# Hyena filters' butterflies in blocks of 64 channels instead of 16, two filter steps per inner tile, and twelve modulation columns beside the output projection

## The chip, the core and the metric

The kernel runs on one core of a Trainium2 chip. The metric is device microseconds from start to end of one execution, the median of several runs. The engines of the core are TensorE (PE, with its weight loads PEld), VectorE (DVE), ScalarE (ACT), GpSimd (POOL) and SyncE (SP). In this kernel SP issues every DMA, in one queue and in its program order (line 50).

## What is computed

One layer of a hybrid diffusion backbone for 1,024 latent and 256 context tokens, width 1,024. The reference, cut to the parts that matter here:

```python
h = x + 1/2 * gate1 * SwiGLU_1(mod1(rms(x)))
h = h + gate2 * W_out[ concat_g norm_g(mixer_g(mod2(rms(h)))) ]   # attention, Hyena, attention, GLA
h = h + 1/2 * gate3 * SwiGLU_2(mod3(rms(h)))
# (shift, scale, gate) x 3 = SiLU(cond) @ W_mod + b_mod : 72 columns of 128 numbers, for latents and for context

def swiglu(x, w_in, w_out):
    a, b = jnp.split(x @ w_in, 2, axis=-1)
    return (jax.nn.silu(a) * b) @ w_out
```

The Hyena mixer is a long convolution by FFT over 256 channels, of order 2. Its filters are implicit: a small MLP of the position gives the taps, and the kernel needs their spectra.

## The kernel before

**Precision and weights.** A product in fp32 is made of three matmuls on operands that are split in a high and a low part (`mm3`, lines 984 to 986: high by high, high by low, low by high). The high part of a weight `wh` is made by ACT (L56), the low part `wl` by POOL or DVE (L62), from a tile `raw` that SP loads. `raw` is a ring of four buffers of 512 KB.

**Stages.** In order of time: `hidden_ctx(0)` and `hidden_lat(0)`, the first half of the first SwiGLU for context and latents; `second(0)`, its second half; projection, Hyena convolution and context attention; linear attention (GLA) and latent attention; the output projection, `w_out(2)` for the context and then `w_out(0)` and `w_out(1)` for the two halves of the latents; then the second SwiGLU with `hidden_ctx(1)`, `hidden_lat(1)` and `second(1)`.

**`hidden_lat`** goes over 22 inner tiles f. Each takes seven products of four chunks by three matmuls of 128x512 (a form of Strassen's: 21 x 4 = 84 matmuls a tile). Between the products DVE adds banks: `u` at L1070, `up1` at L1074 and L1077, `g1` at L1085, and so on. A product that follows in a bank waits for the addition that read it.

**The filters** are a side job of `hidden_lat(0)`: a generator `filters()` from which the loop takes three steps in each inner tile, with high priority. For the latents, after the MLP and the taps, `hyena_spectra` makes four rounds (order `o` by half `g` of 128 channels). A round first makes 8 sub-transforms by matmuls with a DFT matrix (L288, L289), copies and combines them into `sa` and `sd` (ACT L292, DVE L293 and L294), and then runs the butterflies over the 8 sub-transforms, `fft`, in blocks of SW channels. A block takes six operations on POOL (L148 to L153) and ten on DVE (L158 to L163 one each, L166 four), all of which read `sa` and `sd`, and write the block's spectrum to the tile `ks`. That tile has one buffer. It is then stored to `kslat` in DRAM, where each run of SW channels lies by itself. With SW = 16 a round has eight blocks.

**The modulation columns.** `mod_tile(t, sp)` makes column t: it loads 512 KB of `in_wmT`, and DVE multiplies them by SiLU(cond), held in `scb` (1 MB, loaded broadcast and put through a Silu on ACT at L1298), in four accumulating operations (L1311), then adds up (L1313). Columns 16 to 27 are made in `hidden_lat(0)` from f = 10 on, in a pool of one buffer; columns 28 to 71 in `second(0)`. `make_G` and `make_gate` turn columns into the scales and gates that a later stage reads.

**What sets the order.** A scheduler of the framework orders each engine's instructions by priority and dependence. `tc.high_priority(offset=LEAD)` pulls a piece of work ahead of what is written before it; `tc.issue_after(E.last_low)` ties a piece behind the last low split on DVE; `keep_in_program_order` pins an instruction in written order against others of its engine that are pinned. In `w_out` a step loads one weight tile, makes 24 matmuls and evicts the bank with DVE (L1618), which also adds the residual; the result is stored to `hsc2`.

## Time and profile before

| what | value |
|---|---|
| median of 3 runs | 2956.24 us (2952.4 to 2982.59) |
| the profiled execution | 2959.08 us |
| its span in the profile | 2957.3 us |
| mean granted clock of TensorE, share of full speed | 0.961 |
| PE busy | 2749.6 us (93%) |
| PEld busy | 2180.1 us (74%) |
| DVE busy | 1898.0 us (64%) |
| ACT busy | 1133.4 us (38%) |
| POOL busy | 1118.4 us (38%) |
| DMA, mean over the span | 144 GB/s |

Busy shares are means over stages with different limits. PE, busy for 93% of the span, is what the stages mostly wait for, but a stage is only understood from its own rows: how long PE stands still in it, at which granted clock it runs, and which wait ends last. A granted clock of 1.00 is TensorE's level of 2.4 GHz, and a mean below it says that part of the stretch ran at 1.2 GHz.

### The profile page before, as it was taken

The numbers are of one execution on the slowest core, as the hardware profiler recorded it, in microseconds if no ns is written. First come the engines' busy times: TensorE is split into PE (matmuls) and PEld (weight loads), VectorE is DVE, ScalarE is ACT, GpSimd is POOL, SyncE is SP. The second block draws the span as 40 slices with busy tenths as digits, with TensorE's granted clock in tenths as the row PEclk, the third lists the DMA queues.
The fourth block names the chain that finished last, engine by engine and source line by source line (L and its number), as shares of the span: only waits on it lengthen the run. The fifth ranks groups of instructions, "written<-read, shape, count | busy, mean of one in ns | idle before, by whom it ended". The sixth has DMA issues, their size and how long they took to land.

```text
span 2957.3 us, 39868 instructions
## 1 busy us (share of the span) xinstructions
PE 2749.6 (93%) x14088; PEld 2180.1 (74%) x14088; DVE 1898.0 (64%) x3135; ACT 1133.4 (38%) x2051; POOL 1118.4 (38%) x980
## 2 busy tenths in 40 slices
PE   7899988899999888888988989989899999999998
PEld 5886776678788787776754544477898888878888
DVE  4978677754899955767657666662956555533447
ACT  5742222223333642224424434553743333333444
POOL 1334355544000214546415425463435555520002
PEclk9999999999999999899978979999999999999999
DMA  8654755342877563342462110264652222244445
GB/s 296 214 179 139 210 111 125 79 150 93 281 250 263 175 209 113 121 138 84 140 167 50 37 40 12 85 234 157 216 173 97 85 77 84 86 175 149 145 138 202
DMA packets 278460, 427.02 MB, mean 144 GB/s; under 512 B 97417, under 2 KB 163954, under 8 KB 276852
## 3 DMA queue, kind: packets, MB, share of 16 engines
q1 hardware_dynamic: 278260, 424.47, 44.6%
q8 instruction: 111, 1.82, 0.3%
q14 instruction: 89, 0.73, 0.1%
HBM read 345.14 MB, written 79.13 MB: 143 GB/s over the span
## 4 chain that ended last, share of the span: by engine, by line
PE 43%; DVE 5%; DMA 2%; issue 1%; ACT 1%; POOL 1%; SPq 0%; DVEq 0%; POOLq 0%; ACTq 0%
PE ps L986 11%; PE ps L984 10%; PE ps L985 10%; PE ps L740 2%; PE ps L762 1%; PE ps L688 1%; PE ps L763 1%; PE ps L550 1%; PE ps L535 1%; DVE wl L62 1%; DMA gd<-zf 1%; DVE mx L692 1%; PE ps L786 0%; PE ps L546 0%; PE ps L1139 0%
## 5 line engine op out<-in xcount | busy, mean ns | idle before, releaser
L56 ACT ACTIVATE wh<-raw 128x512 fp32r<-128x512 f32 x661 | 408.7, 625 | 513.6 <-PE ps L986 225.0
L62 POOL TENSOR_TENSOR wl<-raw,wh 128x512 fp32r<-128x512 f32 x221 | 328.1, 1489 | 558.1 <-ACT wh L56 342.1
L62 DVE TENSOR_TENSOR wl<-raw,wh 128x512 fp32r<-128x512 f32 x440 | 331.7, 760 | 170.9 <-ACT wh L56 113.2
L985 PE MATMUL ps<-gs,wh 128*128 128x512 f32 (+1 forms) x1056 | 376.5, 357 | 7.0 <-DVE gs L62 7.0
L986 PE MATMUL ps<-gs,wl 128*128 128x512 f32 (+1 forms) x1056 | 373.8, 356 | 2.9 <-DVE wl L62 2.9
L984 PE MATMUL ps<-gs,wh 128*128 128x512 f32 (+1 forms) x1056 | 351.8, 358 | 9.6 <-ACT gs L56 5.0
L984 PE MATMUL ps<-xh,wh 128*128 128x256 f32 (+2 forms) x952 | 320.8, 337 | 12.2 <-ACT zev L1404 5.6
L986 PE MATMUL ps<-xh,wl 128*128 128x256 f32 (+2 forms) x952 | 319.6, 337 | 10.9 <-POOL wl L62 6.4
L985 PE MATMUL ps<-xl,wh 128*128 128x256 f32 (+2 forms) x952 | 323.3, 340 | 0.0
L984 PE MATMUL ps<-t,wh 128*128 128x512 f32 x704 | 281.0, 399 | 11.0 <-DVE up L1077 6.2
L986 PE MATMUL ps<-t,wl 128*128 128x512 f32 x704 | 280.2, 399 | 1.9 <-DVE wl L62 1.9
L985 PE MATMUL ps<-t,wh 128*128 128x512 f32 x704 | 280.5, 398 | 0.0
L984 PE MATMUL ps<-b,wh 128*128 128x512 f32 x528 | 212.6, 403 | 20.6 <-DVE up L1074 19.7
L984 PEld LDWEIGHTS ps<-gs,wh 128*128 128x128 f32 x1056 | 200.3, 190 | 40.7 <-ACT gs L56 5.4
L985 PEld LDWEIGHTS ps<-gs,wh 128*128 128x128 f32 x1056 | 200.9, 190 | 35.9 <-DVE gs L62 7.7
L986 PEld LDWEIGHTS ps<-gs,wl 128*128 128x128 f32 x1056 | 200.5, 190 | 32.4 <-DVE wl L62 3.7
L56 ACT ACTIVATE wh<-s 128x512 fp32r<-128x512 f32 x176 | 110.4, 630 | 295.3 <-PE ps L985 152.1
L985 PE MATMUL ps<-b,wh 128*128 128x512 f32 x528 | 211.5, 401 | 0.0
L986 PE MATMUL ps<-b,wl 128*128 128x512 f32 x528 | 210.9, 399 | 0.2 <-POOL wl L62 0.2
L984 PEld LDWEIGHTS ps<-xh,wh 128*128 128x128 f32 (+1 forms) x952 | 182.3, 192 | 37.5 <-ACT zev L1404 7.2
L986 PEld LDWEIGHTS ps<-xh,wl 128*128 128x128 f32 (+1 forms) x952 | 181.8, 191 | 37.2 <-POOL wl L62 9.1
L919 POOL TENSOR_TENSOR tmp<-tmp 128x512 f32<-128x512 f32 (+1 forms) x18 | 24.7, 1374 | 482.1 <-ACT tmp L917 482.1
(369 smaller groups left out, 5906.5 us busy)
## 6 DMA issues: line engine op xcount, KB each, us to landing
raw<-in_w SPq DMA_DIRECT2D x308, 512.0 KB, 3.5
stg<-in_wmT SPq DMA_DIRECT2D x56, 512.0 KB, 4.1
hid<-g SPq DMA_DIRECT2D x88, 256.0 KB, 2.0
g<-hid SPq DMA_DIRECT2D x88, 256.0 KB, 2.7
m<-in_dft_lat SPq DMA_DIRECT2D x128, 128.0 KB, 2.7
raw<-in_wo SPq DMA_DIRECT2D x24, 512.0 KB, 3.8
x<-in_xT SPq DMA_DIRECT2D x36, 256.0 KB, 4.5
stg<-in_wmp SPq DMA_DIRECT2D x16, 512.0 KB, 10.6
```

The lines of the kernel that those rows point to most:

```text
L56: nc.scalar.activation(out=hi, in_=src, func=ACTF.Copy)
L62: low = eng.tensor_tensor(out=lo, in0=src, in1=hi.bitcast(F32), op=ALU.subtract)
L535: nc.tensor.matmul(ps[:, t], lhsT=kt[32 * h:32 * h + 32, ts], rhs=qt[32 * h:32 * h + 32, ts], start=True, stop=True, tile_position=(32 * h ...
L550: nc.tensor.matmul(ps[:, i0:i0 + 64], lhsT=S[64 * p:64 * p + 64, c], rhs=qt[64 * p:64 * p + 64, 64 * c:64 * c + 64], start=False, stop=c % ...
L688: nc.tensor.matmul(ps, lhsT=qs, rhs=k1[:, lo:hi], start=True, stop=mo is None)
L692: nc.vector.tensor_reduce(out=mx[:, hh * nqt + t, bi:bi + 1], in_=ps, axis=AX.X, op=ALU.max)
L740: mm = nc.tensor.matmul(O[64 * hh:64 * hh + 64, s], lhsT=V[:, kt], rhs=p[hh], start=j == 0, stop=j == last)
L762: nc.tensor.matmul(ps, lhsT=k1[:, ks], rhs=q1[:, hh, a:b], start=True, stop=False)
L763: nc.tensor.matmul(ps, lhsT=k2[:, ks], rhs=q2[:, hh, a:b], start=False, stop=not banded)
L984: nc.tensor.matmul(ps, lhsT=wh(k), rhs=xh(k), start=start and k == 0, stop=False, skip_group_check=loose)
L985: nc.tensor.matmul(ps, lhsT=wh(k), rhs=xl(k), start=False, stop=False, skip_group_check=loose)
L986: nc.tensor.matmul(ps, lhsT=wl(k), rhs=xh(k), start=False, stop=stop and k == nk - 1, skip_group_check=loose)
```

## The change

Blocks of the latents' butterflies have 64 channels, so a round has two blocks instead of eight; an operation is four times as wide, and a store of `ks` has 512 KB in runs of 256 bytes instead of 128 KB in runs of 64. The loop takes two steps of the side job per inner tile instead of three. No modulation columns are made in `hidden_lat(0)`: columns 16 to 59 are made in `second(0)`, 60 to 63 beside `w_out(2)` and 64 to 71 beside `w_out(0)`, from tiles in the ring `raw` that the weights use. For these `scb` is loaded and put through Silu a second time, pinned, ahead of `w_out(2)`. The calls of `make_G` and `make_gate` move accordingly.

```diff
+    def both_conds(p):
+
+        t = p.tile([128, 2, 1024], F32, name="scb")
+        E.load(t, i["cond"].partition_broadcast(128))
+        tc.keep_in_program_order(nc.scalar.activation(out=t, in_=t, func=ACTF.Silu))
+        return t
+
     ms = ExitStack()
     mp = pool(ms, "mp", 1, **R_)
-    scb = mp.tile([128, 2, 1024], F32, name="scb")
-    E.load(scb, i["cond"].partition_broadcast(128))
-    tc.keep_in_program_order(nc.scalar.activation(out=scb, in_=scb, func=ACTF.Silu))
+    scb = both_conds(mp)
...
-    def mod_tile(t, sp):
-
-        w = sp.tile([128, 1024], F32, tag="stg", name="stg")
+    def mod_tile(t, sp, mp=mp, scb=scb, tag="stg"):
+
+        w = sp.tile([128, 1024], F32, tag=tag, name="stg")
...
-    SEQS = (("lat", slice(0, T_LAT), 8, 128, 16), ("ctx", slice(T_LAT, T_ALL), 2, 256, 128))
+    SEQS = (("lat", slice(0, T_LAT), 8, 128, 64), ("ctx", slice(T_LAT, T_ALL), 2, 256, 128))
...
-    sps = ExitStack()
-    sp = pool(sps, "sp", 1, **R_)
     nmod, side_job = 16, filters()
+    nff1 = 60
     for f, _ in enumerate(run):
         with tc.high_priority(offset=LEAD):
-            for _ in range(3):
+            for _ in range(2):
                 next(side_job, None)
-            if f >= 10:
-                mod_tile(nmod, sp)
-                nmod += 1
     for _ in side_job:
         pass
-    sps.close()
...
         for f, _ in enumerate(second(P, 0, c, hid[0], h[c])):
-            if nmod < 72:
+            if nmod < nff1:
                 with tc.issue_after(E.last_low):
                     mod_tile(nmod, sp)
                 nmod += 1
+                if nmod == 24:
+                    make_gate(0)
                 if nmod == 40:
                     make_G(1)
-                    make_gate(0)
-                if nmod == 72:
-                    make_G(2)
-                    make_gate(1)
...
+    mp2 = pool(h2st, "mp2", 1, **R_)
     Y = load_y(2, xp2)
-    for _ in w_out(2, Y, "g", lambda d: h2[:, d]):
+    scb2 = both_conds(mp2)
+
+    def columns(steps, upto):
+
+        nonlocal nmod
+        for t in steps:
+            if nmod < upto:
+                with tc.issue_after(E.last_low):
+                    mod_tile(nmod, P["raw"], mp2, scb2, "raw")
+                nmod += 1
+            yield t
+
+    for _ in columns(w_out(2, Y, "g", lambda d: h2[:, d]), 64):
         pass
+    make_G(2)
...
-            sum_rsq(P, w_out(c, Y[c], "l", lambda d: hq.tile([128, 512], F32, tag="hq", name="hq")), 512, Rl[c],
+            sum_rsq(P, columns(w_out(c, Y[c], "l", lambda d: hq.tile([128, 512], F32, tag="hq", name="hq")), 72), 512, Rl[c],
                     lambda: hq.tile([128, 512], F32, tag="hq", name="rs"))
+    make_gate(1)
```

The following rows show the order of instructions at three places (line of the kernel, operation, out<-in with buffer numbers, shape). A line below the change is a few numbers higher or lower in the new file.

DVE within `hidden_lat(0)`, in the stretch of the butterflies; `u` and `up1` belong to the inner tile, the other names to the filters. Before:

```order
L1074 TENSOR_TENSOR up1_3688<-ps_3647,u_3673 128x512
L163 TENSOR_TENSOR sd_3130<-fP_3593,sd_3130 128x2x16
L166 SCALAR_TENSOR_TENSOR ks_3561<-sd_3130,fA_3570 128x2x16 x2
L166 SCALAR_TENSOR_TENSOR ks_3561<-sd_3130 128x2x16 x2
L158 TENSOR_TENSOR fA_3592<-sd_3130 128x32
L1077 TENSOR_TENSOR up1_3688<-ps_3648,up1_3688 128x512
L159 TENSOR_TENSOR sd_3130<-sd_3130 128x2x16
L162 TENSOR_TENSOR sd_3130<-sd_3130,fP_3593 128x2x16
L160 TENSOR_TENSOR fP_3759<-sd_3130 128x32
L161 TENSOR_TENSOR sd_3130<-sd_3130 128x2x16
L163 TENSOR_TENSOR sd_3130<-fP_3759,sd_3130 128x2x16
L166 SCALAR_TENSOR_TENSOR ks_3583<-sd_3130,fA_3592 128x2x16 x2
```

Now, at the second block of a round:

```order
L159 TENSOR_TENSOR sd_3415<-sd_3415 128x2x64
L163 TENSOR_TENSOR sd_3415<-fP_3834,sd_3415 128x2x64
L162 TENSOR_TENSOR sd_3415<-sd_3415,fP_3834 128x2x64
L62 TENSOR_TENSOR wl_3126<-s4_3123,wh_3125 128x512
L166 SCALAR_TENSOR_TENSOR ks_3824<-sd_3415,fA_3833 128x2x64 x2
L166 SCALAR_TENSOR_TENSOR ks_3824<-sd_3415 128x2x64 x2
L62 TENSOR_TENSOR wl_3130<-raw_3095,wh_3129 128x512
L1070 TENSOR_TENSOR u_3329<-ps_3301,u_3329 128x512
L293 TENSOR_TENSOR sa_3990<-ps_3992,sd_3991 128x2x2x128
L62 TENSOR_TENSOR wl_3270<-s2_3267,wh_3269 128x512
L294 TENSOR_TENSOR sd_3991<-ps_3992,sd_3991 128x2x2x128
L1074 TENSOR_TENSOR up1_3344<-ps_3303,u_3329 128x512
```

The L166 that writes `ks`, which waits for the store of the block before, still stands ahead of the inner tile's L1070 and L1074, but there is one such place in a round and not seven.

PE at the end of the latent attention (L740, L786, and the norm's L801) and the start of `w_out(2)` (L984 to L986, 128x256). Before:

```order
L985 MATMUL ps_17514<-xl_17471,wh_17506 128x256
L986 MATMUL ps_17514<-xh_17470,wl_17507 128x256
L984 MATMUL ps_17514<-xh_17470,wh_17510 128x256
L985 MATMUL ps_17514<-xl_17471,wh_17510 128x256
L786 MATMUL ps_17420<-acc_17249,ones128_87 64x512
L740 MATMUL ps_17251<-p_17405,V_16530 64x512
L740 MATMUL ps_17251<-p_17410,V_16530 64x512
L986 MATMUL ps_17514<-xh_17470,wl_17511 128x256
L984 MATMUL ps_17514<-xh_17470,wh_17510 128x256
L985 MATMUL ps_17514<-xl_17471,wh_17510 128x256
```

And now:

```order
L740 MATMUL ps_16572<-p_16731,V_15851 64x512
L786 MATMUL ps_16741<-acc_16570,ones128_87 64x512
L786 MATMUL ps_16741<-acc_16571,ones128_87 64x512
L801 MATMUL ps_16751<-sq_16752,ones128_87 128x512
L984 MATMUL ps_16841<-xh_16794,wh_16833 128x256
L985 MATMUL ps_16841<-xl_16795,wh_16833 128x256
L801 MATMUL ps_16751<-sq_16755,ones128_87 128x512
L986 MATMUL ps_16841<-xh_16794,wl_16834 128x256
L984 MATMUL ps_16841<-xh_16794,wh_16833 128x256
```

The matmuls of `w_out(2)` stood between those of the attention's last block, and now begin behind all of it. On ACT the cause is seen: the pinned Silu of the second `scb` (L1298), with table loads, stands behind the attention's last work and ahead of the first weight split (L56 of `wh`) of `w_out(2)`:

```order
L789 ACTIVATE r_16744<-ps_16741 128x512
L56 ACTIVATE xh_16794<-yr_16816 128x256
L56 ACTIVATE xh_16794<-yr_16820 128x256
L790 ACTIVATE r_16744<-r_16744 128x512
L56 ACTIVATE xh_16794<-yr_16824 128x256
L800 ACTIVATE sq_16752<-y_16356 128x512
L1298 ACT_TABLE_LOAD
L1298 ACTIVATE scb_16828<-scb_16828 128x2048
L56 ACTIVATE wh_16833<-raw_16831 128x512
```

Before, the splits of those weights stood between the exponentials of the attention's last block, ahead of L789.

SP in `w_out(0)`, the queue of loads and stores. Before:

```order
L50 DMA raw_17971<-in_wo 128x1024
L50 DMA hq_18269<-hsc_83 128x512
L50 DMA hsc2_17465<-h2_17469 128x256 x2
L50 DMA raw_18012<-in_wo 128x1024
L50 DMA hsc2_17465<-h2_17469 128x256
L50 DMA raw_18053<-in_wo 128x1024
```

And now:

```order
L50 DMA raw_17401<-in_wo 128x1024
L50 DMA hsc2_16786<-h2_16790 128x256
L50 DMA stg_17440<-in_wmT 128x1024
L50 DMA hsc2_16786<-h2_16790 128x256
L50 DMA raw_17454<-in_wo 128x1024
L50 DMA stg_17493<-in_wmT 128x1024
```

Between two weight loads there is now a load of a modulation column, into the same ring.

## Rows read from the trace of the kernel before

**Rows 1.** Windows by stage; busy us, clock granted, DMA share, GB/s

```profile
core 0: us, PE busy (x) PEld busy (x) DVE busy (x) ACT busy (x) POOL busy (x), PEclk, DMA share, GB/s
191.00:744.00 553.00, 511.37 (x2188) 401.15 (x2188) 373.97 (x760) 143.56 (x244) 267.70 (x348) 0.97 0.46 131
360.00:580.00 220.00, 189.13 (x842) 152.66 (x840) 159.69 (x408) 50.31 (x88) 121.01 (x238) 0.94 0.47 108
2201.00:2636.00 435.00, 434.90 (x1848) 348.95 (x1848) 229.85 (x247) 136.14 (x228) 231.02 (x152) 1.00 0.25 85
1915.00:1954.00 39.00, 31.02 (x208) 24.66 (x206) 32.74 (x35) 21.57 (x42) 29.36 (x20) 1.00 0.91 324
1954.00:2062.00 108.00, 106.77 (x432) 81.31 (x433) 36.65 (x45) 45.68 (x79) 50.33 (x42) 0.98 0.48 161
```

**Rows 2.** Waits from 191 to 744 us: total us, times, longest us

```profile
POOL ks L150 <- DMA kslat<-ks: 87.7, 23, 8.0
DVE ks L166 <- DMA kslat<-ks: 49.1, 24, 4.7
PE ps L984 <- DVE up L1074: 19.7, 6, 5.0
```

**Rows 3.** Timeline of PE, 394 to 402 us: start, us, line, [idle before <-releaser]

```profile
395.80 0.77 PE L984 MATMUL ps<-b,wh 128*128 128x512 f32 x1 [4.91 <-DVE up L1074]
...
399.56 0.40 PE L984 MATMUL ps<-b,wh 128*128 128x512 f32 x1
```

**Rows 4.** DVE groups by shape, 191 to 744 us: busy, mean ns | idle before

```profile
L1311 DVE SCALAR_TENSOR_TENSOR junk<-stg,scb 128x512 bf16<-128x512 f32 x51 | 40.5, 795 | 17.3 <-DMA stg<-in_wmT 16.6 <-ACT scb L1298 0.4
L166 DVE SCALAR_TENSOR_TENSOR ks<-sd 128x32 f32<-128x32 f32 x64 | 23.8, 409 | 0.0
L166 DVE SCALAR_TENSOR_TENSOR ks<-sd,fA 128x32 f32<-128x32 f32 x64 | 17.6, 315 | 49.1 <-DMA kslat<-ks 49.1
L159 DVE TENSOR_TENSOR sd<-sd 128x32 f32<-128x32 f32 x32 | 16.5, 516 | 0.4
...
L162 DVE TENSOR_TENSOR sd<-sd,fP 128x32 f32<-128x32 f32 x32 | 9.8, 305 | 0.7
...
L1313 DVE SCALAR_TENSOR_TENSOR mod<-part,b_mod 128x2 f32<-128x2 f32 x12 | 4.8, 403 | 0.2
...
L1311 DVE DVE_READ_ACCUMULATOR junk<-stg,scb 128x1 f32 x50 | 3.9, 78 | 0.0
```

**Rows 5.** DVE groups by shape, 1545 to 1915 us

```profile
L557 DVE TENSOR_TENSOR o<-ps,o 128x128 f32<-128x128 f32 x20 | 5.8, 291 | 15.2 <-PE ps L550 15.0
```

**Rows 6.** DMA issues: count, KB each, us to landing

```profile
stg<-in_wmT SPq DMA_DIRECT2D x56, 512.0 KB, 4.1
m<-in_dft_lat SPq DMA_DIRECT2D x128, 128.0 KB, 2.7
raw<-in_wo SPq DMA_DIRECT2D x24, 512.0 KB, 3.8
kslat<-ks SPq DMA_DIRECT2D x32, 128.0 KB, 3.4
scb<-in_cond SPq DMA_DIRECT2D x1, 1024.0 KB, 7.0
```

**Rows 7.** Timeline of ACT at 2019 us, a table load

```profile
2019.14 1.28 ACT L894 ACT_TABLE_LOAD   x1
```

**Rows 8.** ACT groups by shape, 190 to 680 us: the Silu of `scb`

```profile
L1298 ACT ACTIVATE scb<-scb 128x2048 f32<-128x2048 f32 x1 | 1.9, 1922 | 2.2 <-DMA scb<-in_cond 2.2
```

**Rows 9.** Timeline of DVE in `w_out(0)`: two evictions that follow each other

```profile
1994.81 0.75 DVE L1618 SCALAR_TENSOR_TENSOR hq<-ps,mod,hq 128x512 f32<-128x512 f32 x1 [5.72 <-PE ps L986]
2001.28 0.75 DVE L1618 SCALAR_TENSOR_TENSOR hq<-ps,mod,hq 128x512 f32<-128x512 f32 x1 [5.71 <-PE ps L986]
```

**Rows 10.** Timeline of POOL at 1920 us: eight low splits in a row

```profile
1920.32 12.26 POOL L62 TENSOR_TENSOR wl<-raw,wh 128x512 fp32r<-128x512 f32 x8
```

## Prediction, made before the changed kernel had run

> **What bounds the kernel now.** I read the windows view by stage first, because a share of the whole span mixes stages with different limits. The same kind of stage stands there twice [rows 1]: `hidden_lat(0)`, with the filters beside it, from 191 to 744 us (553.0 us), and `hidden_lat(1)`, without them, from 2201 to 2636 us (435.0 us). Both hold the same 1,848 matmuls of the three-product chain; the second has PE busy for 434.90 of its 435.00 us at a granted clock of 1.00. So without a side job the stage is purely PE's. In the first the surplus is 118 us. It splits as follows: PE idle 553.00 − 511.37 = 41.6 us; clock 0.97 instead of 1.00, that is 0.03 × 553 = 16.6 us; the rest, some 60 us, is the filters' own matmuls, which the change leaves as they are. What the change can give back in this stage is therefore at most 41.6 + 16.6 = 58 us.
>
> Where is the idle time? From 360 to 580 us PE is idle for 220.00 − 189.13 = 30.9 us and the clock is 0.94 [rows 1]. This is where the filters' butterflies run. The waits view gives the cause [rows 2]: DVE waits 24 times, 49.1 us in all, for the store `kslat<-ks` to leave the only `ks` tile, and PE waits 19.7 us in 6 long stalls for DVE's `up` (L1074). The timeline shows one link of it [rows 3]: PE stands still for 4.91 us in front of a matmul that needs `up`. DVE itself is busy 159.7 of these 220 us and stands 49.1 us at `ks`: 208.8 of 220. So here DVE sets the pace, a third of it by waiting, and PE pays 30.9/49.1 = 0.63 us for each us of that wait.
>
> **The change, part by part.**
>
> *Wider blocks.* A block of 16 channels costs DVE ten operations, 320 for 32 blocks. The two L166 rows have 23.8 + 17.6 us, the six rows L158 to L163 (16.5 us the dearest, 9.8 the cheapest) 69.8: together 111 us [rows 4]. With 64 channels there are 8 blocks, 80 operations of 128 columns. The trace has a DVE operation of that size at 291 ns [rows 5], no dearer than the narrow ones at 305 to 516: what is paid here is paid per instruction. So 80 × 0.29 = 23 us, and 80 × 0.516 = 41 us if the strided forms stay dear. DVE is relieved of 70 to 88 us; POOL in proportion, but it waits 87.7 us for the same store [rows 2] and nobody waits for it.
>
> *The waits on `ks`.* One of the blocks in each round now shares the tile with the one before it, so the waits fall from 24 to about 4 (the second block of each of 4 rounds; the first has a whole round of matmuls ahead of it). A wait now has a mean of 49.1/24 = 2.05 us, 1.35 less than the landing of 3.4 us [rows 6]. The new store is four times as large, 512 KB in 2,048 runs of 256 bytes, where the old has 128 KB in 2,048 runs of 64. Small runs cost little in these rows: 128 KB in few long runs (`m<-in_dft_lat`) takes 2.7 us, and 512 KB in long runs 3.8 to 4.1. I take 4.1. Four waits of 4.1 − 1.35 = 2.75 us are 11 us of DVE, and by 0.63 that is 7 us of PE. In order, the waiting L166 now stands ahead of L1070 and L1074 in one of the places shown, so what waits behind it is again `u` and `up`, and PE behind them: the wait is rarer, not harmless. PE's other idle time in the stage, 41.6 − 30.9 = 10.7 us, I leave as it is. So 41.6 − 7 − 10.7 = **24 us** gained.
>
> Beside this stands a rule. The Trainium skill ("DMA: Bandwidth & Descriptors", section "Specifications") states a minimum transfer of 512 bytes for line rate, below which the DMA engine reads, modifies and writes; the new 256-byte runs are still below it. The rows speak against a large effect (64-byte runs cost 0.7 us more than long ones at 128 KB), but no transfer of 512 KB in such runs is in the trace; what it would mean is the second rival, and the sum by it 2961 us.
>
> *Clock.* The matmul right behind the stall of [rows 3] takes 0.77 us, one 3.76 us later 0.40 us: PE runs slower for some microseconds after it has stood still. Over the stretch the granted clock is 0.94, against 1.00 in the undisturbed stage [rows 1]. With about a sixth of the waits I expect half of the 16.6 us back, **8 us**; the bounds are 0 and 16.6.
>
> *The twelve columns.* One takes four products of 0.795 us, four accumulator reads of 0.078 and one of 0.403, so 3.9 us of DVE [rows 4], 47 us for twelve. They leave the last 12 of the 22 tiles of `hidden_lat(0)`, where they stand beside and behind the butterflies; that helps DVE there, but what PE can gain by it is already counted in the idle time. They come back at the output projection.
>
> *Side job at two steps a tile.* The filters come to 65 steps before (24 blocks more) and 41 after; at three a tile the first fill 21.7 of the 22 tiles, at two the second 20.5. So the spread over the tiles stays as it was, PE's work too, and I cost it at nothing; without that room, steps left over would run with no matmuls of the tiles beside them, at most the 60 us of the filters' own. `second(0)` makes 44 columns in both kernels, numbered differently: nothing.
>
> *Output projection for the context (`w_out(2)`, 1915 to 1954 us).* The DMA already moves 324 GB/s at a share of 0.91 [rows 1]. Added are the second load of the conditioning, 1 MB, and four columns of 512 KB: 3.1 MB, 9.7 us at that rate. At the same time ACT gets a pinned Silu of 1.92 us [rows 8] and three more table loads of 1.28 us [rows 7], 5.8 us in front of the first weight split, and order shows that matmuls of `w_out(2)` no longer fill the tail of the attention. If both lie side by side the price is the larger; if PE covers all but the table loads it is 3.8, and one after the other it is 15.5. I take **9.7 us**: the row has a DMA that is nearly full.
>
> *Output projection for the latents.* Eight columns are 31 us of DVE in the 54 us of `w_out(0)`, where DVE now has about half of 36.65 us in 108 [rows 1]: 49 of 54, tight but under. An eviction (L1618) comes every 6.47 us, and DVE waits 5.7 us ahead of it [rows 9]; a column of 3.9 us fits in that gap. The DMA goes from 161 GB/s to about 240, under the 324 just seen. I take **3 us** (0 to 8).
>
> *Sum*, against the profiled execution's 2959.08 us: −24 − 8 + 9.7 + 3 = −19.3, so 2939.8. The median of the runs is 2956.24, 2.8 lower; on its scale that is **2937 us**.
>
> **The rivals.**
>
> *The stage gains nearly everything.* If the waits that are left fall where DVE has room, idle time and clock come back but for some 6 us: 58 − 6 = 52 gained, 13 lost, so 2956 − 39 = 2917. For it speaks that DVE's load falls by over 110 us, against it that the waiting L166 stands ahead of L1074.
>
> *The large store is slow.* If the landing grows with the bytes at small runs, it takes 4 × 3.4 = 13.6 us. Four waits of 13.6 − 1.35 = 12.2 us are 49 us again, exactly what DVE waits now; the stage then keeps its idle time and its clock and gains only what DVE's relief gives elsewhere, between 0 and 24 (I take 8, as DVE waits rather than works in those stalls). 2956 + 13 − 8 = 2961. It is the time that the Trainium skill's rule on small transfers, named above, would bring. Against it: 2.7, 3.8 and 4.1 us in [rows 6].
>
> *The other side: the shared ring at the output projection.* The columns are loaded into the same ring of four buffers as the weights of `w_out`, and SP issues in order: a column's buffer that DVE hasn't yet read holds back the next weight load and all behind it. With two buffers for weights a load has two steps, 2 × 6.47 = 12.9 us, less its landing of 4.1 [rows 6]; once DVE is more than 8.8 us late, each of the 8 steps waits for a landing: 8 × 4.1 = 33 us. Loss 9.7 + 3 + 33 = 46 against 32 gained: 2956 + 14 = 2970. For it: DVE is 49 of 54 us full, and POOL needs 1.53 us for each half of a weight [rows 10] before that buffer is free. Against it: the eviction has 5.7 us of room, so lateness doesn't add up.
>
> *Order's remainder.* The scheduler also arranges the latent attention and the linear attention beside it differently; the trace gives that no price, so it only widens the range by some 5 us either way.
>
> **How the numbers follow.** The sum's case 0.50, with its own range of 2923 to 2951 (idle and clock terms 15 to 45 together, the output projection 4 to 20); nearly everything gained 0.22; the slow store 0.14; the ring 0.14. The predicted time is that of the first. The range must leave out no more than 2 in 10: it runs from 2908 (lower third of the second case left out) to 2969 (about half of the ring case and the top of the slow store left out). A measurement of this kernel can tell about 1%, 29.6 us, from no change: faster means under 2926.7, slower over 2985.8. Faster: 0.9 of the 0.22, and a quarter of the 0.50, so 0.32. Slower: 0.4 of the ring case, if more than the 8 steps wait, and 0.2 of the slow store, if waits grow beyond those of now: 0.08. Within: 0.60.
>
> **What would show it.** Right: DVE's waits on `ks` fall from 24 to about 4 and from 49 to near 11 us; `kslat<-ks` lands in about 4 us; the DVE operations of L158 to L166 are near 0.3 us; PE idle in `hidden_lat(0)` is near 18 us at a clock of 0.98 or 0.99; the stretch of `w_out(2)` is some 10 us longer, that of `w_out(0)` some 3. Wrong: a landing above 10 us (slow store); PE waiting on `wh` or `raw<-in_wo` at each step of `w_out(0)` (ring); an idle time in `hidden_lat(0)` under 10 us (all gained); or a difference in stages where order shows none.

## The result and the profile after

The changed kernel takes **2923.41 us** (median of 4 runs, 2915.49 to 2929.44). Against the runs of the kernel before the ratio is 0.988, with a 95% interval of 0.985 to 0.991: some 1.2% faster. I had forecast 2937, with 2908 to 2969. The range held and so did the direction, but 13.6 us too little was forecast, and the stages show that this small miss is the difference of larger ones. By the bound that the prediction set itself (faster means under 2926.7 us) the result is "faster", which had 0.32, and not "within", which had 0.60.

The stages as the timelines give them, from the first or last matmul of one to that of the next (profiled executions, spans 2957.3 and 2922.5 us):

| stage | before | after | difference | forecast |
|---|---|---|---|---|
| `hidden_lat(0)` with the filters | 555.6 | 502.2 | −53.4 | −32 |
| `second(0)` | 326.6 | 331.2 | +4.6 | 0 |
| projection, Hyena, context attention | 404.4 | 398.7 | −5.7 | 0 |
| linear and latent attention, first to last L740 | 442.2 | 419.2 | −23.0 | 0 (±5) |
| last L740 to the first matmul of `hidden_lat(1)` | 281.2 | 321.9 | +40.7 | +12.7 |
| `hidden_lat(1)` and `second(1)` | 742.7 | 742.4 | −0.3 | 0 |

The 4.6 and −5.7 us of the second and third rows nearly cancel; where they come from was not looked into.

The windows of the changed kernel that answer to [rows 1] (columns as there): `hidden_lat(0)`, `hidden_lat(1)`, and the stretch after the attention in two pieces.

```profile
193.00:696.00 503.00, 492.54 (x2189) 392.57 (x2190) 284.82 (x418) 146.17 (x245) 244.55 (x205) 1.00 0.42 130
...
2165.00:2602.00 437.00, 434.63 (x1848) 349.00 (x1848) 231.02 (x251) 137.59 (x229) 231.10 (x152) 1.00 0.25 85
...
1852.00:1900.00 48.00, 28.40 (x146) 24.43 (x147) 41.79 (x69) 28.78 (x44) 22.01 (x15) 0.68 0.94 345
1900.00:1955.00 55.00, 46.14 (x200) 35.94 (x199) 54.30 (x98) 22.86 (x45) 35.81 (x28) 0.90 0.56 184
```

In `hidden_lat(0)` PE is now idle for 10.5 us, not 41.6, and the clock is 1.00. In the stretch of `w_out(2)` it is the other way round: PE is busy for 28.40 of 48 us, at a clock of 0.68, with DVE busy for 41.79.

The waits of the changed kernel in `hidden_lat(0)`, which answer to [rows 2] (us in total, times, longest):

```profile
DVE ks L166 <- DMA kslat<-ks: 6.4, 4, 2.7
```

The 24 waits are 4, as forecast, and take 6.4 us where I had put 11; PE's stalls on `up` (L1074), 6 before and 19.7 us, are one of 2.5 us. The store lands in 5.1 us, where I had taken 4.1 (DMA issues: count, KB each, us to landing, as in [rows 6]):

```profile
stg<-in_wmT SPq DMA_DIRECT2D x56, 512.0 KB, 3.7
raw<-in_wo SPq DMA_DIRECT2D x24, 512.0 KB, 4.8
...
kslat<-ks SPq DMA_DIRECT2D x8, 512.0 KB, 5.1
```

### The profile page after: what moved, and what is told of

Read it like the earlier page. It is cut to its first block, busy times and chain, and to the rows that moved or that the text cites. A ratio compares the mean times of both kernels' runs of the same rounds, so it can differ in the third digit from the quotient of the medians.

```text
span 2922.5 us, 39427 instructions
## 1 busy us (share of the span) xinstructions
PE 2732.5 (93%) x14088; PEld 2176.7 (74%) x14088; DVE 1851.9 (63%) x2895; ACT 1143.4 (39%) x2055; POOL 1087.7 (37%) x836
## 4 chain that ended last, share of the span: by engine, by line
PE 42%; DVE 6%; DMA 2%; ACT 1%; issue 1%; SPq 1%; POOL 0%; DVEq 0%; ACTq 0%; POOLq 0%
PE ps L986 11%; PE ps L984 10%; PE ps L985 10%; PE ps L740 2%; DVE junk L1316 2%; PE ps L688 1%; PE ps L762 1%; PE ps L763 1%; SPq L50 1%; PE ps L550 1%; PE ps L535 1%; DMA stg<-in_wmT 1%; PE ps L546 0%; PE ps L786 0%; DMA q<-ml 0%
## 5 line engine op out<-in xcount | busy, mean ns | idle before, releaser
L56 ACT ACTIVATE wh<-raw 128x512 fp32r<-128x512 f32 x661 | 407.9, 625 | 541.6 <-PE ps L986 242.9
L986 PE MATMUL ps<-gs,wl 128*128 128x512 f32 (+1 forms) x1056 | 376.3, 358 | 2.0 <-DVE wl L62 2.0
L984 PE MATMUL ps<-gs,wh 128*128 128x512 f32 (+1 forms) x1056 | 353.8, 359 | 8.7 <-ACT gs L56 5.0
L984 PE MATMUL ps<-xh,wh 128*128 128x256 f32 (+2 forms) x952 | 325.7, 342 | 18.0 <-DVE mod L1318 8.3
L986 PE MATMUL ps<-xh,wl 128*128 128x256 f32 (+2 forms) x952 | 323.9, 341 | 8.6 <-DVE wl L62 6.8
L984 PE MATMUL ps<-t,wh 128*128 128x512 f32 x704 | 278.4, 395 | 4.5 <-ACT wh L56 4.5
L986 PE MATMUL ps<-t,wl 128*128 128x512 f32 x704 | 277.6, 395 | 0.0
L56 ACT ACTIVATE wh<-s 128x512 fp32r<-128x512 f32 x176 | 110.7, 632 | 309.3 <-PE ps L985 150.5
L984 PEld LDWEIGHTS ps<-gs,wh 128*128 128x128 f32 x1056 | 200.2, 191 | 40.6 <-ACT gs L56 5.2
L62 DVE TENSOR_TENSOR wl<-s,wh 128x512 fp32r<-128x512 f32 x132 | 120.2, 911 | 172.1 <-PE ps L985 95.6
L986 PEld LDWEIGHTS ps<-gs,wl 128*128 128x128 f32 x1056 | 200.8, 191 | 32.1 <-DVE wl L62 2.6
L984 PEld LDWEIGHTS ps<-xh,wh 128*128 128x128 f32 (+1 forms) x952 | 185.8, 195 | 43.4 <-ACT wh L56 12.5
L984 PE MATMUL ps<-b,wh 128*128 128x512 f32 x528 | 208.3, 394 | 2.5 <-DVE up L1074 2.5
L986 PEld LDWEIGHTS ps<-xh,wl 128*128 128x128 f32 (+1 forms) x952 | 184.5, 194 | 33.5 <-DVE wl L62 8.8
L985 PE MATMUL ps<-b,wh 128*128 128x512 f32 x528 | 208.8, 395 | 0.0
L986 PE MATMUL ps<-b,wl 128*128 128x512 f32 x528 | 208.5, 395 | 0.0
```

Source lines behind the costliest of these rows:

```text
L56: nc.scalar.activation(out=hi, in_=src, func=ACTF.Copy)
L62: low = eng.tensor_tensor(out=lo, in0=src, in1=hi.bitcast(F32), op=ALU.subtract)
L984: nc.tensor.matmul(ps, lhsT=wh(k), rhs=xh(k), start=start and k == 0, stop=False, skip_group_check=loose)
L985: nc.tensor.matmul(ps, lhsT=wh(k), rhs=xl(k), start=False, stop=False, skip_group_check=loose)
L986: nc.tensor.matmul(ps, lhsT=wl(k), rhs=xh(k), start=False, stop=stop and k == nk - 1, skip_group_check=loose)
```

## The experiments

They take the three stages that moved apart: which part of the change gave the 53 us, where the 23 come from, and what the 41 at the output projection consist of. Stages of all runs, in us, measured as in the table above:

| run | `hidden_lat(0)` | attention | last L740 to `hidden_lat(1)` | median | ratio to before (95%) |
|---|---|---|---|---|---|
| before | 555.6 | 442.2 | 281.2 | 2959.2 | |
| the change | 502.2 | 419.2 | 321.9 | 2923.4 | 0.988 (0.985 to 0.991) |
| columns moved, 16 channels | 538.8 | 418.5 | 321.1 | 2962.1 | 1.002 (0.999 to 1.005) |
| 32 channels, columns in place | 521.8 | 433.2 | 282.5 | 2923.2 | 0.988 (0.984 to 0.993) |
| 64 channels, columns late | 516.8 | 433.7 | 282.5 | 2911.3 | 0.986 (0.980 to 0.992) |
| the change, 56 columns in `second(0)` | 502.0 | 430.9 | 294.4 | 2921.0 | 0.988 (0.983 to 0.992) |
| the change, loads only | 502.7 | 434.3 | 303.8 | 2920.4 | 0.989 (0.984 to 0.994) |
| the change, products only | 503.1 | 420.9 | 311.2 | 2910.1 | 0.987 (0.982 to 0.993) |
| the change, no second Silu | 505.1 | 417.5 | 318.7 | 2925.1 | 0.990 (0.987 to 0.993) |
| 64 channels, columns split 4 and 8 | 507.0 | 445.2 | 287.9 | 2921.0 | 0.989 (0.987 to 0.990) |
| 64 channels, columns late, behind the low split | 502.7 | 434.0 | 282.1 | 2897.8 | 0.981 (0.977 to 0.985) |
| 64 channels, twelve columns left out | 502.6 | 440.4 | 281.4 | 2897.1 | 0.980 (0.977 to 0.983) |
| the change once more | 503.9 | 420.7 | 324.2 | 2924.7 | 0.990 (0.987 to 0.993) |

Each ratio is against runs of the kernel before on the same chip; the stages are those of one profile each. Wide blocks with the columns where they were is not among the runs. What wide blocks give without columns is the difference of two rows, the columns moved with 16 channels and the change: 538.8 − 502.2 = 36.6 us. They differ in the steps per tile too, which the run without columns shows to make no difference.

**Columns moved, with the second conditioning that they need, and nothing else.**

```diff
-    SEQS = (("lat", slice(0, T_LAT), 8, 128, 64), ...
+    SEQS = (("lat", slice(0, T_LAT), 8, 128, 16), ...
-            for _ in range(2):
+            for _ in range(3):
                 next(side_job, None)
```

(against the changed kernel)

> The kernel before with the twelve columns moved and nothing else: blocks of 16 channels, three steps per tile. Theory (three separate terms: wider blocks -53 us in hidden_lat(0), a different order of the attention -21, the columns +37 at the output projection): the attention stands in the same order as in the changed kernel, so it is some 20 us shorter; the output projection some 37 us longer; hidden_lat(0) at most 10 us shorter, since the 24 waits on ks are all still there; in all 2965 us (2955 to 2975). Rival (what helped hidden_lat(0) is that the columns left it): hidden_lat(0) 25 us shorter or more, in all under 2950.

Measured 2962.1 us, no difference from before that can be told. The attention is 23.7 us shorter and the output projection 39.9 longer, both as the theory had it. `hidden_lat(0)` is 16.8 us shorter, between the two forecasts. The waits on `ks` there stand almost as before, the stalls on `up` are fewer (us in total, times, longest):

```profile
DVE ks L166 <- DMA kslat<-ks: 43.8, 23, 4.3
PE ps L984 <- DVE up L1074: 10.6, 4, 3.5
```

So the columns' leaving has a share of its own in the 53 us: 16.8. Where it comes from is seen in the trace of the kernel before. The program makes these columns from f = 10 on, but with the high priority of the side job they run much earlier (products by tile, 191 to 700 us: ns least, median and most, first and last start):

```profile
L1311 DVE SCALAR_TENSOR_TENSOR junk<-stg,scb x48: 671/684/1776, 200.8 to 319.7; 128x512 bf16<-128x512 f32 x48
```

That is in the first six of the 22 inner tiles, and the first operation of a butterfly starts behind it, at 351 us. The same 70 us of the stage, 29 us after its start, in the kernel before and with the columns moved (columns as in [rows 1]):

```profile
220.00:290.00 70.00, 63.07 (x237) 45.68 (x236) 58.06 (x109) 16.66 (x29) 31.37 (x21) 0.98 0.41 136
```

```profile
223.50:293.50 70.00, 70.00 (x259) 49.12 (x257) 40.23 (x55) 17.88 (x30) 27.76 (x22) 1.00 0.40 128
```

PE is idle for 6.9 us beside the columns and for none without them. Over the whole stage its idle time falls from 44.2 to 32.5 us and its busy time, for the same matmuls, from 511.4 to 506.4. The other 5 us of idle time go later in the stage, where no column ran; why is open. For the whole kernel the moved columns by themselves win nothing.

**Blocks of 32 channels, columns where they were.**

```diff
-    SEQS = (("lat", slice(0, T_LAT), 8, 128, 16), ...
+    SEQS = (("lat", slice(0, T_LAT), 8, 128, 32), ...
```

> The kernel before with blocks of 32 channels; the columns stay where they were, three steps per tile. Theory (the number of waits on ks and of operations sets the loss): 12 waits in place of 24, 160 operations in place of 320; hidden_lat(0) 25 to 40 us shorter, attention and output projection as before, in all 2925 us. Rival (the columns' leaving is what helps): under 15 us shorter, 2945 or more.

Measured 2923.2 us, `hidden_lat(0)` 33.8 us shorter: the theory. DVE's waits on `ks` are 16.4 us in 9 times, where 12 times were expected. One number changed gives as much as the whole change, since nothing is paid at the output projection.

**Blocks of 64, columns late in `hidden_lat(0)`.**

```diff
-    SEQS = (("lat", slice(0, T_LAT), 8, 128, 16), ...
+    SEQS = (("lat", slice(0, T_LAT), 8, 128, 64), ...
...
             for _ in range(3):
-                next(side_job, None)
-            if f >= 10:
-                mod_tile(nmod, sp)
-                nmod += 1
+                done = next(side_job, True)
+            if done and sp is None:
+                sp = pool(sps, "sp", 2, **R_)
+            for _ in range(2 if sp is not None else 0):
+                if nmod < 28:
+                    mod_tile(nmod, sp)
+                    nmod += 1
```

(against the kernel before, in part; in the loop over the inner tiles, with its high priority; the output projection as before)

> Blocks of 64 channels, three steps per tile; the twelve columns stay in hidden_lat(0), but two per tile behind the last step of the filters, in a pool of two buffers that is opened then; nothing is made at the output projection. Theory: hidden_lat(0) about 50 us shorter than before, since DVE has room in tiles without filters (47 us of columns in some 8 tiles of 20 us, of which DVE has 10 free each); the attention stands in the order of before and takes as long as before; the output projection as before; in all 2909 us (2900 to 2915). Rival (columns beside the inner tiles cost PE time wherever they are): hidden_lat(0) at most 30 us shorter, 2930 or more.

Measured 2911.3 us, output projection and attention as in the run with 32 channels. The total is the theory's; `hidden_lat(0)`, at 516.8 us, misses its 505 and is 14.6 longer than in the changed kernel, 1.2 us a column. What they do there is seen in the run with the columns behind the low split.

**All 56 columns in `second(0)`, second conditioning kept.**

```diff
-    nff1 = 60
+    nff1 = 72
```

(against the changed kernel, as are the next three)

> The changed kernel with all 56 columns in second(0), none at the output projection; the second conditioning is still loaded and put through its pinned Silu. Theory: the output projection loses at most 10 us against before (Silu, its table loads, 1 MB) where it lost 37; second(0), where DVE has 285 us of 325 and gets 47 more, is 10 to 30 us longer; in all 2905 to 2925 us. Rival (the Silu and the attention tail that is no longer filled are the loss): the output projection still 25 us or more longer than before, in all over 2930.

Measured 2921.0 us. Without a column beside it, the stretch behind the attention is still 13.2 us longer than before, a little more than the 10 expected, and 27.5 shorter than in the changed kernel. So the second conditioning costs about 13, the columns about 27. What the move into `second(0)` saves there is paid elsewhere: `second(0)` is 8.7 us longer than before, and the stage behind it 7.0. The attention stands in an order of its own here, and 40 us of it ran at a mean clock of 0.62 (1804 to 1844 us).

**Loads only, and products only.** In the first the four products of the twelve columns are left out, in the second their loads:

```diff
+        if tag == "raw":
+            w = sp.tile([128, 1024], F32, tag=tag, name="stg")
+            E.load(w, i["wmT"][t - 16])
+            nc.vector.scalar_tensor_tensor(out=mod[:, t], in0=w[:, 0:2], ...)
+            return
```

```diff
+        if tag == "raw":
+            w = scb.rearrange("p c k -> p (c k)")[:, :1024]
+        else:
...
```

> The changed kernel with the four products of each of the twelve columns at the output projection left out: the 512 KB are loaded into the shared ring as before, and one small operation reads them, so these columns are not the real ones. From the last L740 to the start of hidden_lat(1) the kernel before takes 281 us, the changed one 322, and one with the second conditioning and no columns 294. Theory (DVE: its products, four to a column, stand ahead of the evictions and of the low splits): 295 to 302 us, in all 2900 us. Rival (ring and DMA: a column's load takes a weight's buffer): 312 to 322 us, in all 2918 us.

> The changed kernel with the loads of the twelve columns at the output projection left out: the products are made on data that is already there (the second conditioning), so these columns are not the real ones, and the ring holds weights alone. Theory (DVE): 312 to 322 us from the last L740 to hidden_lat(1), in all 2918 us. Rival (ring and DMA): 294 to 302 us, in all 2900 us. About 305 here and in the run with loads alone would say that it takes both.

Measured 303.8 us with loads alone and 311.2 with products alone, where 294.4 is the stretch with the conditioning only and 321.9 the whole. So the loads cost 9.4, the products 16.8, together 26.2 of 27.5: it takes both, nearly as a sum, the products the larger part. Neither theory holds alone. The medians can't show these parts, as the four runs of each kernel scatter over 31 and 36 us; they rest on one profile each, and the changed kernel's own stretch came out 2.3 us apart in two profiles.

**The Silu left out.**

```diff
-    scb2 = both_conds(mp2)
+    scb2 = both_conds(mp2, False)
```

> The changed kernel with the second Silu left out (the conditioning is loaded and used as it is, so twelve columns are not the real ones). It tells what the pinned Silu with its table loads costs, beside the loads. Theory (the tail of the attention can be filled again and two table loads go): 322 - 8 = 314 us from the last L740 to hidden_lat(1), in all 2915 us. Rival (the columns behind it are the bound, the Silu is hidden in front of them): 320 us or more, in all 2922 us.

Measured 318.7 us for the stretch, 3.2 shorter; the median, 2925.1, can't be told from the changed kernel's. The stretch lies between the theory's 314 and the rival's 320, nearer the rival: the Silu itself is nearly hidden. By difference some 10 of the 13 us are left for the 1 MB load and for the tail of the attention, which `w_out(2)` doesn't fill in this run either; the two were not taken apart.

**Columns split, four late in `hidden_lat(0)`, eight in `hidden_lat(1)`.**

```diff
+    for f, _ in enumerate(hidden_lat(P, 1, XL, hid[1])):
+        if 4 <= f and nmod < 72:
+            with tc.high_priority(offset=LEAD):
+                mod_tile(nmod, sp2, mp2, scb2)
...
```

(the part in `hidden_lat(1)`; four columns late as above)

> A version meant to be faster than both: blocks of 64 channels, three steps per tile; four columns late in hidden_lat(0), 44 in second(0), and the last eight (gate 3, not read until second(1)) in hidden_lat(1), which has DVE busy for 230 us of 435 and a DMA share of 0.25, with a conditioning of its own. Against the run with all twelve late in hidden_lat(0), 2911 us, theory (columns are free where DVE has room and no load shares a ring with weights): hidden_lat(0) 8 to 10 us shorter, hidden_lat(1) at most 3 longer, in all 2903 us. Rival (a column costs PE time beside inner tiles wherever it stands, 1.2 us each): as in that run, 2911 us or more.

Measured 2921.0 us; this version was meant to win and doesn't. `hidden_lat(0)` is 507.0, as expected, but `hidden_lat(1)` 445.7, 12 longer: 1.5 us a column. PE waits 6.8 us there for `up`, where it waited for nothing before. The rival: with high priority a column costs PE time beside inner tiles also where DVE is busy for only half the stage. The attention, in yet another order, is 11.5 us longer than in the run with all twelve late.

**Columns late, but behind the last low split.**

```diff
-            for _ in range(2 if sp is not None else 0):
-                if nmod < 28:
-                    mod_tile(nmod, sp)
-                    nmod += 1
+        for _ in range(2 if sp is not None else 0):
+            if nmod < 28:
+                with tc.issue_after(E.last_low):
+                    mod_tile(nmod, sp)
+                nmod += 1
```

(against the run with the columns late; now outside the high priority)

> As the run with twelve columns late in hidden_lat(0), but each column is issued behind the last low split on DVE and not with the high priority of the side job, so that its four products are spread between the splits. There hidden_lat(0) was 516.8 us, 14.6 more than without columns. Theory (a column costs where its four products stand in a row ahead of an addition that PE waits for): hidden_lat(0) 503 to 508 us, in all some 2900 us. Rival (it is DVE's time or the load that counts, not the place): hidden_lat(0) 514 us or more, in all 2909 to 2915 us.

Measured **2897.8 us**, the fastest kernel of the study that makes all columns, 0.9% under the changed one and 1.9% under the one before. `hidden_lat(0)` is 502.7 us: the theory. PE's waits in the tiles with columns, first with high priority (500 to 708 us), then behind the low split (500 to 694 us):

```profile
PE ps L986 <- DVE wl L62: 6.6, 3, 2.2
PE ps L984 <- DVE up L1074: 1.4, 2, 0.7
```

```profile
PE ps L984 <- issue: 2.8, 1, 2.8
```

And the windows of these two stretches (the late columns with high priority, then behind the low split):

```profile
500.00:708.00 208.00, 197.23 (x842) 160.79 (x840) 136.32 (x226) 61.91 (x104) 96.64 (x66) 0.98 0.35 113
```

```profile
500.00:694.00 194.00, 191.23 (x845) 158.05 (x844) 140.84 (x230) 61.49 (x104) 98.87 (x67) 1.00 0.37 122
```

DVE does the same work, even a little longer (140.84 against 136.32 us). What is gone is PE's wait for a low split `wl` that stood behind a column's products, 8 us of idle, and the clock's dip to 0.98.

**Twelve columns left out.**

```diff
-                    mod_tile(nmod, sp)
+                    nc.vector.tensor_copy(mod[:, nmod], bmod[:, 0:2])
```

(in the kernel with the columns late)

> As the run with twelve columns late in hidden_lat(0), but these twelve are left out (a copy of two numbers stands in their place), so those columns are not the real ones. It gives what the wider blocks bring with no column to pay for. Theory: hidden_lat(0) 502 us as in the changed kernel, the attention in the order of before, output projection 281 us, in all 2896 us. Rival (the two steps per tile have a share in hidden_lat(0)): 508 us or more with three steps, in all over 2902 us.

Measured 2897.1 us, `hidden_lat(0)` 502.6 with three steps per tile: two steps or three makes no difference. The run before it, with all columns, is as fast as this one without: the twelve columns cost nothing there.

**The change once more**, without an edit.

> The changed kernel once more, for what differs from one execution to another. Theory (the order of the attention gives its length, up to a stretch of some 40 us at half clock that comes in some executions, 13 us): attention 417 to 421 us, or 431 to 436 with such a stretch; hidden_lat(0) 501 to 505; output projection 318 to 323; in all 2923 us, times scattered over 15 us. Rival (nothing scatters, the 15 us between runs in the same order come from their code): every stage within 2 us of the first profile.

Measured 2924.7 us. `hidden_lat(0)` and the attention fall in the forecast bounds, the output projection is 1.2 us above them. The four times scatter over 14.6 us, as the theory had it, but the single stages of the two profiles repeat within 2.3 us, close to the rival; the step from `w_out(2)`'s last eviction to `w_out(1)`'s is the exception (114.5 us against 110.8).

## Why the prediction held, and where its sum was off

**The waits on `ks`: right.** Their number fell as worked out (24, 9 and 4 times at 16, 32 and 64 channels), DVE's loss from 49.1 over 16.4 to 6.4 us, and PE's idle time with it. The rival of the slow store is out: 128, 256 and 512 KB, in runs of 64, 128 and 256 bytes, land in 3.4, 3.8 and 5.1 us. The Trainium skill's minimum of 512 bytes ("DMA: Bandwidth & Descriptors", section "Specifications") lies above the runs of the old store as well as those of the new one. Against loads of 512 KB in long runs (3.7 and 4.8 us) the new store is 0.3 to 1.4 us slower, and not four times as slow; no store in long runs was measured.

**The gain in `hidden_lat(0)`: 32 us forecast, 53.4 measured. What failed is the term that was put at nothing.** Over the whole stage PE's idle time is 44.2 us before, 32.5 with the columns alone moved, and 10.2 in the changed kernel; its busy time 511.4, 506.4 and 492.0. So the wide blocks gave 22 us of idle time, where I had 24: this term was right in kind and in size. With it came 14 us of busy time at a higher clock, where I had 8. The other 16.8 us belong to the columns' leaving, which I put at nothing, since "what PE can gain by it is already counted in the idle time". I had the columns in the last 12 of the 22 tiles, beside and behind the butterflies, as the program writes them. The trace that I had shows them in the first six, and 6.9 of the 10.7 us of idle time outside the butterflies, which I left as it was, stood beside them. In all, the stage gained what the rival "the stage gains nearly everything" had, 52; that rival doesn't name the columns either.

**The price of a wide butterfly operation: wrong, without effect.** I took 0.29 us from [rows 5]. The 80 operations take 49.6 us, 0.62 on average (DVE groups by shape, first and last of eight; columns as in [rows 4]):

```profile
L166 DVE SCALAR_TENSOR_TENSOR ks<-sd 128x128 f32<-128x128 f32 x16 | 12.0, 787 | 0.0
...
L158 DVE TENSOR_TENSOR fA<-sd 128x128 f32<-128x128 f32 x8 | 2.6, 329 | 0.0
```

My row is the price of an operation that POOL doesn't disturb: it reads one of its operands, `ps`, from PSUM. The butterflies read two from SBUF, mostly beside POOL. One of L158 to L163 takes 0.28 us in each of the 24 cases in which POOL has nothing running, and 0.86 on average in the 24 in which it has (last section). DVE's relief is 62 us, not 70 to 88. As DVE no longer sets the pace, nobody paid for it.

**The output projection: the term that was mis-sized most, 12.7 instead of 40.7.** The part of `w_out(0)` and `w_out(1)` was right (3 forecast; 107.7 before, 110.8 after). `w_out(2)` was put at 9.7 and cost 35.8 (last L740 to its last eviction: 32.1 before, 67.9 after). I priced the added DMA, and let it hide the rest. The runs give: second conditioning 13, loads 9, products 17, which add rather than hide one another. What I missed is that DVE is short there too. With products only, PE waits longest until DVE has evicted a bank, behind products; with loads only, until a weight is split (waits of PE, us in total, times, longest: products only, 1855 to 1900 us; loads only, 1868 to 1915 us):

```profile
PE ps L984 <- DVE h L1619: 9.6, 2, 5.4
```

```profile
PE ps L984 <- ACT wh L56: 10.2, 2, 9.1
```

The longest stall of the changed kernel is of the second kind, in the timelines of SP, POOL, ACT and PE (start us, us, engine, line, [idle before <-releaser]):

```profile
1870.42 0.33 SPq L50 DMA_DIRECT2D raw<-in_wo  x1
...
1884.66 2.45 SPq L50 DMA_DIRECT2D raw<-in_wo  x2
```

```profile
1873.24 3.03 POOL L62 TENSOR_TENSOR wl<-raw,wh 128x512 fp32r<-128x512 f32 x2 [3.24 <-ACT wh L56]
```

```profile
1890.70 2.19 ACT L56 ACTIVATE wh<-raw 128x512 fp32r<-128x512 f32 x4 [1.00 <-DMA raw<-in_wo]
```

```profile
1891.39 0.58 PE L984 MATMUL ps<-xh,wh 128*128 128x256 f32 x1 [8.30 <-DVE mod L1318]
```

Between 1870.42 and 1884.66 SP issues no weight. The next one is split at 1890.70, and PE starts after 8.30 us of standing still. Two of the ring's four buffers hold columns in this time, as the rival of the shared ring has it, but they don't hold back this weight. The buffer whose turn it is held the weight whose low splits POOL ends at 1876.27, SP shows no wait for POOL, and in the run with loads only, where a column is read at once, the same gap is 15.1 us long. Sixteen other transfers stand between in SP's order, and SP waits 7.6 us for earlier ones to land (waits of SP, 1871 to 1892 us):

```profile
SPq L50 <- DVE mod L1318: 4.4, 2, 2.5
SPq L50 <- DMA hq<-hsc: 2.6, 6, 1.1
SPq L50 <- DMA raw<-in_wo: 2.2, 2, 1.3
SPq L50 <- DMA stg<-in_wmT: 1.9, 2, 1.0
SPq L50 <- DMA yr<-ysc: 0.9, 3, 0.3
```

Only two of the weights behind it wait until DVE has read a column (first row, 4.4 us). So the rival's mechanism is there in small part, and in `w_out(2)`, not, as I had it, in `w_out(0)`. How the loads' 9 us divide between the shared ring and a DMA that is busy for 0.94 of this stretch is open. Idle time is not all of it: from 1852 to 1900 us PE is idle for 19.6 us and the granted clock is 0.68, so the matmuls that do run are slow as well.

**A product's price was low too.** 48 products at the output projection have a mean of 1.09 us, where [rows 4] had 0.795; a column takes (52.2 + 3.8 + 4.9)/12 = 5.1 us of DVE, not 3.9 (DVE groups by shape, 1840 to 2060 us):

```profile
L1316 DVE SCALAR_TENSOR_TENSOR junk<-stg,scb 128x512 bf16<-128x512 f32 x48 | 52.2, 1087 | 5.8 <-ACT sq L800 4.9
L1318 DVE SCALAR_TENSOR_TENSOR mod<-part,b_mod 128x2 f32<-128x2 f32 x12 | 4.9, 405 | 0.2
L1316 DVE DVE_READ_ACCUMULATOR junk<-stg,scb 128x1 f32 x48 | 3.8, 78 | 0.0
```

**The attention: not priced, 23 us.** I let the scheduler's other order there widen the range by 5 us. The runs separate it: in the order of the kernel before it took 442.2, 433.2, 433.7, 434.0 and 440.4 us, in that of the changed kernel 419.2, 418.5, 420.9, 417.5, 420.7 and once 434.3. (The runs with 56 columns in `second(0)` and with columns split have orders of their own.) Some 3 us of this are, by estimate, 16 matmuls of `w_out(2)` that stood inside it before. Some 9 in the two profiles compared are the clock (below). The remaining 11 or so go with the order, and the run with only the columns moved has them too, so it isn't the wider blocks. Which place of the order makes them is open; no run changes it alone.

So the one mechanism that I worked out held, but the total came near by luck: two gains of 21 and 23 us that I didn't see were met by 28 of losses that I didn't see.

## What to carry to other kernels

When one engine paces a stage by waiting for a single buffer, count the waits and not the operations: blocks of 32 instead of 16 took them from 24 to 9, and this one number brought as much as the whole change. Look in the trace where a piece of work stands before you price its leaving; the program doesn't tell it where a scheduler sets the order. Work that is moved out of a busy stage has to be priced where it lands, on every engine there, and added up rather than taken as the largest of parts. Before moving it, try another place in the order of the same engine: the twelve columns cost 14.6 us in front of the low splits and nothing behind them.

## What the runs showed of the hardware

**DVE's operations on two SBUF tiles beside POOL.** The same product of two SBUF tiles takes 0.68 to 0.69 us in each of the 20 cases at the output projection in which POOL has nothing running, and 1.37 on average, up to 1.78, in the 28 that overlap with a POOL operation. A product and, 1.6 us later, an operation that reads PSUM instead, both beside the row of POOL's splits below them; the second keeps its 0.68 us:

```profile
1864.01 1.65 DVE L1316 SCALAR_TENSOR_TENSOR junk<-stg,scb 128x512 bf16<-128x512 f32 x1
...
1865.59 0.68 DVE L75 TENSOR_SCALAR rs<-ps 128x512 f32<-128x512 f32 x1
```

```profile
1860.46 6.34 POOL L62 TENSOR_TENSOR wl<-raw,wh 128x512 fp32r<-128x512 f32 x4 [13.10 <-ACT wh L56]
```

The Trainium skill says why ("SBUF — State Buffer", section "Who interferes with whom"): a VectorE instruction with two SBUF inputs contends with a GpSimd instruction that reads SBUF; one with at most one SBUF input, outside the 2-port perf modes, doesn't. These rows agree, and so do the butterflies above (0.28 us without POOL, 0.86 beside it). A price for such a DVE operation has to be taken from a stretch with the same work on POOL.

**The clock in the attention differs between profiles in the same order.** Stretches of 40 us in the same order and place (columns as in [rows 1]): the kernel before, and the run with 32 channels; then the run with loads only, and the changed kernel.

```profile
1717.60:1757.60 40.00, 35.74 (x146) 18.90 (x144) 30.56 (x58) 10.35 (x23) 9.93 (x10) 0.63 0.06 21
```

```profile
1680.00:1720.00 40.00, 34.79 (x181) 18.66 (x181) 32.54 (x64) 11.83 (x26) 14.66 (x13) 0.87 0.06 21
```

```profile
1778.00:1818.00 40.00, 38.54 (x137) 18.85 (x136) 21.59 (x35) 9.79 (x20) 11.52 (x9) 0.66 0.05 16
```

```profile
1785.40:1825.40 40.00, 38.35 (x192) 19.26 (x190) 26.65 (x44) 16.04 (x32) 12.15 (x10) 1.00 0.05 16
```

PE is busy for nearly the same time in each pair, but at 0.63 and 0.66 a larger part of the stretch ran at 1.2 GHz, and fewer matmuls were done (146 against 181, 137 against 192). The attention as a whole took some 7 to 15 us longer in the three profiles with such a stretch than in the others of the same order, so a difference of one profile against one other is not worth more than that in this stage. These are profiles of different kernels; the two of the changed kernel both lack the stretch. That one kernel differs from run to run shows in its total alone: the four runs with products only went from 2905.9 us at a mean clock of 0.967 to 2941.9 us at 0.955.
